# Feed-forward output projection by block products: seven for eight, in four chunks

## The chip, the core and the metric

The kernel runs on one core of a Trainium2 chip. The metric is device microseconds of one launch, lower is better; the number for a version is the median over several runs. A profile is one further execution, recorded by the hardware profiler.

## What is computed

One layer of a decoder: attention (MLA) over a prompt of 512 tokens and a batch of 8 single-token samples with paged caches, a chunked gating mixer, an output projection `w_o`, then the feed-forward part, then a gated per-layer embedding. Weights are shared by the two groups, and the kernel puts both side by side as 520 token columns. What the change touches is the last line of `conv_ffn`:

```python
def conv_ffn(hn, hist, w_ff_in, conv_w, conv_b, w_ff_out):
    a = hn @ w_ff_in                      # 1024 -> 2 x 2816
    ap = jnp.concatenate([hist, a], axis=1)
    c = conv_b
    for k in range(CONV_W):               # three taps along the tokens
        c = c + conv_w[k] * ap[:, k:k + T]
    g, up = c[..., :D_FF], c[..., D_FF:]
    return (jax.nn.silu(g) * up) @ w_ff_out, ...   # 2816 -> 1024
...
    h = h + f
    gate = sigmoid(rmsnorm(h) @ w_ple_gate)        # 1024 -> 1024
    e = rmsnorm(p_emb @ w_ple_proj)                # 256 -> 1024
    h = h + gate * e
```

All data are float32.

## The kernel before

**Layout.** Activations stand transposed: features on the 128 partitions, the 520 tokens as columns, in two halves of 260 (`HT`). The residual `x` is four tiles of two feature blocks each, so eight blocks `m`. `D_FF` is 22 tiles of 128 (`NFF`).

**Three matmuls for one.** Each float32 operand is split into a high part (cast to the type fp32r of the profile rows) and a low part (the rest): `split` (line 132 and after) makes the high part on ScalarE (line 135, or 137 with a scale) and the low part by a subtraction on VectorE (line 130, or 143 with a scale). `mm3` (lines 145 to 148) then adds high x high, high x low and low x high into the same PSUM tile: three matmuls of 128 x 128 weights by 260 columns.

**Weights.** `wq_add` puts every weight block of the kernel into one list of units, in the order of use. `wload` brings a unit from memory into one of three raw buffers `WR` by a DMA on SyncE's queue (line 190). `wget(i)` returns unit i split into two `W` tiles (there are nine), and beforehand splits the units up to three further ahead. So eight `W` tiles are in use or made ready.

**Feed-forward.** The 22 tiles of `D_FF` are taken in thirds of 8, 8 and 6 (`THIRDS`, line 907). For each tile f of a third, two input projections (gate and up: 48 matmuls each) run by `proj`; `ff_half` (line 1054) evacuates one with the normaliser (line 1057), convolves it (ScalarE line 1059, VectorE lines 1060 to 1062); the SiLU is line 1097, the product with up line 1098, and the result is split as the right-hand operand of the output projection (line 1099). After the last tile of a third the output projection runs over its tiles: for each of eight blocks m a `proj` of nf k-tiles (nf x 6 matmuls), added into `x[m]` from PSUM by VectorE (line 1111). The first two blocks leave out their last k-tile until both are otherwise done (`proj_two`), which gives the last activation time.

**End section.** In the last third three `e_mm` (the embedding projection, 12 matmuls each, copied out on ScalarE at line 1077 and squared for a norm, line 217, added up by VectorE at line 221) come ahead of the output projection, and the other five between its blocks. Behind each add into `x[m]` the finished block is split for the gate projection with a scale (lines 137, 143) and squared for its norm. The gate stage follows: eight projections of 48 matmuls, the last in two column halves into PSUM tiles of their own (`proj_apart`), with evacuation at line 1137.

**PSUM.** `mm()` tiles hold two banks (three tiles), `ms()` tiles one bank (two tiles).

**Order.** The code names the engine of each operation. The tile framework plans the order of each engine's instructions at build time: an instruction whose inputs come later by the plan may be overtaken by one that is written behind it. At run time each engine takes its instructions in the planned order, and waits on semaphores. A tile from a ring (`W`, `WR`, PSUM) can be written again once all readers of its earlier content have finished.

**GpSimd** works earlier, in the attention stages, among them on the rotary products of lines 466 to 469, which VectorE and GpSimd share by token blocks, and on low parts of the cache pages (line 130 with GpSimd as its engine). It has no work in the feed-forward.

Of the kernel before, what the change touches and what calls it, by code (L numbers as in the profile page):

```python
# [8 lines left out]
F32R = mybir.dt.float32r  # L9
# [11 lines left out]
NT = T + B  # L21
# [9 lines left out]
NFF = 22  # L31
# [8 lines left out]
NAT = 8  # L40
KRQ = 2
EF = 3
PF = 2
# [3 lines left out]
def trunk_step(ctx: ExitStack, tc: tile.TileContext, I, O):  # L47
# [125 lines left out]

    wunits = []
    wraw = []
    wsrc = {}
    wtiles = []

    def wq_add(src, w, l="v", scale=None, tile_=W, parts=1):

        cuts = [(i * w // parts, (i + 1) * w // parts) for i in range(parts)]
        wunits.append((src, l, scale or [None] * parts, tile_, cuts))
        return len(wunits) - 1

    def wload(i):
        while len(wraw) <= i:
            src, _, _, _, cuts = wunits[len(wraw)]
            wraw.append(WR())
            for a, b in cuts if len(wraw) == 1 else [(0, cuts[-1][1])]:
                nc.sync.dma_start(wraw[-1][:, a:b], src[:, a:b])  # L190

    def wget(i, ahead=3):
        while len(wtiles) < min(i + 1 + ahead, len(wunits)):
            n = len(wtiles)
            wload(n)
            _, l, scale, tile_, cuts = wunits[n]
            wh, wl = tile_(F32R), tile_(F32R)
            for (a, b), sc in zip(cuts, scale):
                split(wh[:, a:b], wl[:, a:b], wraw[n][:, a:b], scale=sc, l=l)
            wsrc[n], wraw[n] = wraw[n], None  # L200
            wtiles.append((wh, wl))
        return wtiles[i]
# [703 lines left out]

    THIRDS = [(0, 8), (8, 8), (16, 6)]
    k_o = [wq_add(I["w_o"][i], 1024) for i in range(8)]
    k_fi, k_fo, k_pp = {}, {}, {}
    for th, (f0, nf) in enumerate(THIRDS):  # L910
        for f in range(f0, f0 + nf):
            for m in (f, NFF + f):
                k_fi[m] = wq_add(I["w_ffi"][m], 1024)
        for m in range(8):
            if th == 2 and m in (0, PF):
                k_pp[m > 0] = wq_add(I["w_pp"][int(m > 0)], 1024)
            k_fo[th, m] = wq_add(I["w_ffo"][th][m], nf * 128)
    k_pg = [wq_add(I["w_pg"][m], 1024) for m in range(8)]
# [18 lines left out]
    def halves(v):  # L937
        return v.rearrange("p (b t) -> p b t", b=2)
# [114 lines left out]

    def ff_half(m, ps):
        a = abuf[acnt[0] % NA]
        acnt[0] += 1
        nc.vector.tensor_mul(halves(a[:, 2:]), ps[:, :, 0:HT], halves(rstd_b))  # L1057
        c = A()
        nc.scalar.activation(c[:, 0:T], a[:, 2:T + 2], AF.Identity, scale=cw[:, m, 2:3], bias=cw[:, m, 3:4])  # L1059
# [9 lines left out]
    def e_mm(m):  # L1069
# [8 lines left out]
        ne.add(e[m])  # L1078

    hph, hpl = [], []  # L1080
    for th, (f0, nf) in enumerate(THIRDS):
        acth, actl = pair(nf // 2, F32R), pair(nf // 2, F32R)
        for f in range(nf):
            if th == 2 and f == 3:
# [5 lines left out]
            ks = k_fi[f0 + f], k_fi[NFF + f0 + f]  # L1090
            pg, pu = proj_two(ks, hn, 8) if f0 + f == 0 else (proj(k, hn, 8) for k in ks)
            if f0 + f == 0:
                nc.scalar.preload_act_table_set("natural_log_exp_and_others")
                nf_.finish(rstd_b)
            g = ff_half(f0 + f, pg)
            u_ = ff_half(NFF + f0 + f, pu)
            nc.scalar.activation(g, g, AF.Silu)
            nc.vector.tensor_mul(g, g, u_)  # L1098
            split(acth[f // 2][:, f % 2], actl[f // 2][:, f % 2], g)
        if th == 2:  # L1100
            for m in range(EF):
                e_mm(m)

        def act(kt):
            return acth[kt // 2][:, kt % 2], actl[kt // 2][:, kt % 2]

        first = proj_two([k_fo[th, m] for m in range(2)], act, nf)
        for m in range(8):
            ps = first[m] if m < 2 else proj(k_fo[th, m], act, nf)
            xv = x[m // 2][:, m % 2]  # L1110
            nc.vector.tensor_add(halves(xv), halves(xv), ps[:, :, 0:HT])
            if th == 2:
                if m % 2 == 0:
                    hph += pair(1, F32R)
                    hpl += pair(1, F32R)
                split(hph[m // 2][:, m % 2], hpl[m // 2][:, m % 2], xv, scale=g_pl[:, m:m + 1])
                np_.add(xv)
                if m + EF < 8:
                    e_mm(m + EF)
    nc.sync.dma_start(O["conv"], convb)  # L1120
# [23 lines left out]
def _layout(inp):  # L1144
# [63 lines left out]
    wo = g["w_ff_out"][0]  # L1208
    for i, (f0, nf) in enumerate([(0, 8), (8, 8), (16, 6)]):
        a[f"w_ffo{i}"] = tiles(wo[f0 * 128:(f0 + nf) * 128]).reshape(8, 128, nf * 128)  # L1210
    pe = np.concatenate([g["p_prompt"][0, 0], g["p_sample"][0, :, 0]], 0)
# [35 lines left out]
```

## Time and profile before

| | |
|---|---|
| runs, median (lowest to highest of 3) | 922.03 us (921.96 to 923.37) |
| profiled execution | 920.34 us, of which the span 918.6 |
| TensorE clock granted, mean | 0.99 |
| feed-forward with its end section | 560 to 868 us of the span |
| thirds' output projections | about 570.5 to 616.6, 708.9 to 755.2, 824 to 867 |
| gate stage | 868 to 918.6 |

How to read it: a profile row names an engine, a source line of the kernel before, the operation, `output<-inputs` by the program's tile names, the shapes, and how often. On the timeline the first two numbers are the start (us from the span's start) and the duration; in brackets stands how long the engine had been idle before it, and what it waited for. PE is TensorE (PEld its weight loads), DVE VectorE, ACT ScalarE, POOL GpSimd, SP SyncE. A matmul is shown for longer than the distance to the next, since matmuls are pipelined; the distance of starts is what counts.

### The profile page before, as it was taken

How to read it: one execution, taken by the hardware profiler on the slowest of the kernel's cores; microseconds unless marked ns; L12 is line 12 of the kernel's file. 1: busy time of each engine (PE TensorE's matmuls, PEld its weight loads, DVE VectorE, ACT ScalarE, POOL GpSimd, SP SyncE). 2: the span in 40 equal slices, each digit the busy share in tenths (PEclk: the TensorE clock that was granted, in tenths of full speed). 3: DMA queues.
4: the chain of work that ended last, by engine and by line, in shares of the span. 5: the costliest groups of instructions: out<-in, count | busy, mean ns of one | idle time of the engine just before them, and what ended most of it. 6: DMA issues, size and time to landing. Idle time of an engine off the chain costs nothing.

```text
span 918.6 us, 20633 instructions
## 1 busy us (share of the span) xinstructions
PE 892.9 (97%) x7799; PEld 846.5 (92%) x7799; DVE 660.2 (72%) x1133; ACT 503.0 (55%) x1188; POOL 204.7 (22%) x208
## 2 busy tenths in 40 slices
PE   7998999999999999989999999999999999999997
PEld 5896878888898888979999999999999999999997
DVE  6579766669999999897668776337776337776775
ACT  6573368777877787864446443224444214455561
POOL 5004841127676667630000000000000000000000
PEclk9998999999999999989999999999999999999999
DMA  6332150352667556314233222322222222323311
GB/s 217 99 96 81 50 182 1 95 161 79 203 183 210 161 162 193 121 31 138 86 100 110 89 86 86 103 89 87 90 93 92 93 92 93 104 85 98 116 58 59
DMA packets 65204, 100.44 MB, mean 109 GB/s; under 512 B 13825, under 2 KB 47754, under 8 KB 65106
## 3 DMA queue, kind: packets, MB, share of 16 engines
q1 hardware_dynamic: 63058, 94.93, 32.3%
q0 software_dynamic: 2048, 4.20, 1.8%
q8 instruction: 62, 1.02, 0.5%
q14 instruction: 36, 0.29, 0.1%
HBM read 95.95 MB, written 3.15 MB: 108 GB/s over the span
## 4 chain that ended last, share of the span: by engine, by line
PE 82%; DVE 7%; ACT 3%; DMA 2%; issue 2%; SPq 2%; POOL 1%; DVEq 0%; ACTq 0%
PE mm L146 24%; PE mm L148 24%; PE mm L147 23%; DVE ss L752 2%; PE ms L816 2%; PE ms L693 2%; SPq L601 1%; POOL xs L280 1%; DMA u<-pages 1%; DVE g L157 1%; DMA a<-xT 1%; PE ms L153 1%; PE mm L678 1%; PE ms L641 1%; PE mm L658 1%
## 5 line engine op out<-in xcount | busy, mean ns | idle before, releaser
L146 PE MATMUL mm<-u,w 128*128 128x260 f32 x1392 | 395.2, 284 | 0.0
L148 PE MATMUL mm<-u,w 128*128 128x260 f32 x1392 | 394.3, 283 | 0.0
L147 PE MATMUL mm<-u,w 128*128 128x260 f32 x1392 | 393.4, 283 | 0.0
L148 PEld LDWEIGHTS mm<-u,w 128*128 128x128 f32 x1392 | 262.0, 188 | 0.3 <-issue 0.2
L147 PEld LDWEIGHTS mm<-u,w 128*128 128x128 f32 x1392 | 262.1, 188 | 0.2
L146 PEld LDWEIGHTS mm<-u,w 128*128 128x128 f32 x1392 | 261.8, 188 | 0.4 <-PE mm L148 0.2
L130 DVE TENSOR_TENSOR w<-wr,w 128x1024 fp32r<-128x1024 f32 (+1 forms) x94 | 112.8, 1201 | 104.2 <-issue 54.3
L752 DVE TENSOR_REDUCE ss<-sq 128x8 f32<-128x512 f32 x256 | 166.6, 679 | 14.1 <-ACT sq L750 12.2
L750 ACT ACTIVATE sq<-mm 128x512 f32<-128x512 f32 x256 | 153.6, 614 | 34.7 <-PE mm L148 21.1
L135 ACT CAST w<-wr 128x1024 fp32r<-128x1024 f32 (+1 forms) x94 | 96.5, 1031 | 138.1 <-PE mm L148 127.3
L146 PE MATMUL mm<-wuk,a 128*128 128x260 f32 x416 | 124.8, 300 | 3.9 <-ACT raw L751 3.4
L148 PE MATMUL mm<-wuk,a 128*128 128x260 f32 x416 | 119.0, 286 | 0.0
L147 PE MATMUL mm<-wuk,a 128*128 128x260 f32 x416 | 118.6, 285 | 0.0
L146 PEld LDWEIGHTS mm<-wuk,a 128*128 128x128 f32 x416 | 79.4, 191 | 7.8 <-ACT raw L751 6.4
L147 PEld LDWEIGHTS mm<-wuk,a 128*128 128x128 f32 x416 | 79.6, 191 | 0.0
L148 PEld LDWEIGHTS mm<-wuk,a 128*128 128x128 f32 x416 | 79.4, 191 | 0.0
L588 POOL DMA_INDIRECT wr<-krT,idx x64 | 62.1, 971 | 11.4 <-issue 6.3
L1059 ACT ACTIVATE a<-abuf,cst 128x512 f32<-128x512 f32 x44 | 35.9, 816 | 39.3 <-DVE abuf L1057 39.2
L1060 DVE SCALAR_TENSOR_TENSOR a<-abuf,cst,a 128x512 f32<-128x512 f32 x44 | 33.1, 752 | 25.4 <-ACT a L1059 25.1
L130 POOL TENSOR_TENSOR a<-u,a 128x512 fp32r<-128x512 f32 x34 | 45.5, 1339 | 25.8 <-ACT a L714 13.0
L751 ACT COPY raw<-mm 128x8 f32<-128x8 f32 x256 | 45.9, 179 | 0.0
L135 ACT CAST u<-a 128x520 fp32r<-128x520 f32 x24 | 14.8, 626 | 43.4 <-DVE a L1098 43.3
(306 smaller groups left out, 1339.3 us busy)
## 6 DMA issues: line engine op xcount, KB each, us to landing
wr<-w_ffi SPq DMA_DIRECT2D x44, 512.0 KB, 3.3
u<-pages SPq DMA_DIRECT2D x152, 128.0 KB, 2.3
w<-pages SPq DMA_DIRECT2D x104, 128.0 KB, 2.4
wr<-w_ffo SPq DMA_DIRECT2D x16, 512.0 KB, 3.3
wr<-w_o SPq DMA_DIRECT2D x8, 512.0 KB, 4.3
wr<-w_pg SPq DMA_DIRECT2D x8, 512.0 KB, 3.2
wr<-w_ffo SPq DMA_DIRECT2D x8, 384.0 KB, 3.4
a<-xT SPq DMA_DIRECT2D x8, 260.0 KB, 7.2
```

The lines of the kernel that those rows point to most:

```text
L130: return (nc.vector if eng == "v" else nc.gpsimd).tensor_sub(dl, src, dh.bitcast(F32))
L135: nc.scalar.copy(dh, src)
L146: nc.tensor.matmul(out, lh, rh, start=start, stop=False)
L147: nc.tensor.matmul(out, lh, rl, start=False, stop=False)
L148: return nc.tensor.matmul(out, ll, rh, start=False, stop=stop)
L588: nc.gpsimd.indirect_dma_start(krT[:, g * 128:(g + 1) * 128], None, I["krT"], bass.IndirectOffsetOnAxis(ap=idx.bitcast(U32)[:, b * 8 + g:b ...
L693: nc.tensor.matmul(po[:, 0:256], v[:, ks], pt_[:, k * 256:k * 256 + 256], start=(k == 0), stop=(k == qb))
L750: squares.append(nc.scalar.activation(u3(sq, 2, 256), ps[:, :, 0:256], AF.Square))
L751: nc.scalar.copy(raw[:, c * 8:c * 8 + 8].rearrange("p (a h) -> p a h", a=2), ps[:, :, 256:260])
L752: nc.vector.tensor_reduce(ss[:, c * 8:c * 8 + 8], sq.rearrange("p (h d) -> p h d", d=DN), axis=AX.X, op=ALU.add)
L1059: nc.scalar.activation(c[:, 0:T], a[:, 2:T + 2], AF.Identity, scale=cw[:, m, 2:3], bias=cw[:, m, 3:4])
L1060: nc.vector.scalar_tensor_tensor(c[:, 0:T], a[:, 1:T + 1], cw[:, m, 1:2], c[:, 0:T], op0=ALU.mult, op1=ALU.add)
```

## The change

The output projection is written as 2 x 2 block products. The left operand of a quad q is the weights of two output blocks (m = 2q, 2q + 1) by pairs of k-tiles, the right operand the activations of such pairs by the two column halves. Strassen's scheme in Winograd's form gets the four result blocks from seven products: with the weight blocks A11, A21, A12, A22 it uses A11, S1 = A21 + A22, S2 = S1 - A11, S3 = A11 - A21, A12, A22, S4 = A12 - S2, and on the right B11, T1, T2, T3, B21, T4, B22.

- The 22 tiles are taken in chunks of 6, 6, 6 and 4 (`CHUNKS`).
- Weights: a quad has two loads and seven units of cost 1 (one `W` tile holds high and low part, half a width each); the other units have cost 2. `wget` looks ahead up to a cost of 8. The sums S1 to S4 run on GpSimd (six-tile chunk: 384 columns each, four-tile chunk: 256), into the `sq` ring of three tiles.
- Right-hand operand: class `Right` gets each finished activation; for a pair of tiles it makes four differences on GpSimd (260 columns each) and splits seven operands. It lies in up to eight `U` tiles and in `G` tiles.
- Results: each product has a PSUM bank of its own, `ms` for the products P0, P2 and P6, `mm` for the others. ScalarE copies the first, VectorE adds six of them up by seven additions of 260 columns, and four further additions into `x` run on GpSimd.
- The first tile of the next chunk (`ahead`) is projected ahead of the chunk's products, and its convolution and product run between the quads.
- In the last chunk the split of `x`, its norm and the `e_mm` follow each quad, two blocks at a time. `w_ff_out` is stored in the new order ahead of the launch.

```diff
+QUAD = ("A11", "S1", "S2", "S3", "A12", "A22", "S4")
+CHUNKS = ((0, 6), (6, 6), (12, 6), (18, 4))
...
+        def make(name):
+            a = wraw[n]
+            b = wraw[n + 1] if name != "A11" else None
+            a11, a21 = a[:, 0:w], a[:, w:2 * w]
+            if name[0] == "A":
+                v = a11 if name == "A11" else b[:, 0:w] if name == "A12" else b[:, w:2 * w]
+            else:
+                v = s[name] = Q()[:, 0:w]
+                if name == "S1":
+                    nc.gpsimd.tensor_add(v, a21, b[:, w:2 * w])
+                elif name == "S2":
+                    nc.gpsimd.tensor_sub(v, s["S1"], a11)
+                elif name == "S3":
+                    nc.gpsimd.tensor_sub(v, a11, a21)
+                else:
+                    nc.gpsimd.tensor_sub(v, b[:, 0:w], s["S2"])
+            t = W(F32R)
+            wh, wl = t[:, 0:w], t[:, w:2 * w]
+            split(wh, wl, v)
...
-    def wget(i, ahead=3):
-        while len(wtiles) < min(i + 1 + ahead, len(wunits)):
+    def wget(i, ahead=None):
+        while len(wtiles) < len(wunits):
             n = len(wtiles)
...
+            make, ld, cost = wunits[n]
+            if n > i and (n > i + ahead if ahead is not None else sum(u[2] for u in wunits[i:n + 1]) > 8):
+                break
+            wload(ld)
+            wtiles.append(make())
...
+        def add(self, g):
+            lo, hi = slice(0, HT), slice(HT, NT)
+            if self.g is None:
+                self.g = g
+                self.put("B11", g[:, lo])
+                nc.gpsimd.tensor_sub(g[:, lo], g[:, hi], g[:, lo])
+                self.put("T1", g[:, lo])
+                return
+            p, self.g = self.g, None
+            self.put("B21", g[:, lo])
+            self.put("B22", g[:, hi])
+            nc.gpsimd.tensor_sub(p[:, hi], g[:, hi], p[:, hi])
+            nc.gpsimd.tensor_sub(p[:, lo], g[:, hi], p[:, lo])
+            self.put("T2", p[:, lo])
+            nc.gpsimd.tensor_sub(g[:, lo], g[:, lo], p[:, lo])
+            self.put("T3", p[:, hi])
+            self.put("T4", g[:, lo])
+
+    def products(k, right, x0, x1):
...
+        def prod(i, name, ps):
+            wh, wl = wget(k + i)
+            ops = right.ops[name]
+            for kt, (rh, rl) in enumerate(ops):
+                ks = slice(kt * 128, kt * 128 + 128)
+                mm3(ps[:, 0:HT], wh[:, ks], wl[:, ks], rh, rl, kt == 0, kt == len(ops) - 1)
+
+        t, c = A(), A()
+        p1, u2 = t[:, lo], t[:, hi]
+        ps1, pa = ms(), mm()
+        prod(0, "B11", ps1)
+        nc.scalar.copy(p1, ps1[:, 0:HT])
+        nc.gpsimd.tensor_add(x0[:, lo], x0[:, lo], p1)
+        prod(1, "T1", pa[:, 0])
+        ps6 = ms()
+        prod(2, "T2", ps6)
+        nc.vector.tensor_add(u2, ps6[:, 0:HT], p1)
+        nc.vector.tensor_add(c[:, lo], pa[:, 0, 0:HT], u2)
+        nc.gpsimd.tensor_add(x0[:, hi], x0[:, hi], c[:, lo])
+        prod(3, "T3", pa[:, 1])
+        nc.vector.tensor_add(u2, pa[:, 1, 0:HT], u2)
+        nc.vector.tensor_add(c[:, hi], pa[:, 0, 0:HT], u2)
+        nc.gpsimd.tensor_add(x1[:, lo], x1[:, lo], u2)
+        nc.gpsimd.tensor_add(x1[:, hi], x1[:, hi], c[:, hi])
+        pb = mm()
+        prod(4, "B21", pb[:, 0])
+        nc.vector.tensor_add(x0[:, lo], x0[:, lo], pb[:, 0, 0:HT])
+        prod(5, "T4", pb[:, 1])
+        nc.vector.tensor_add(x1[:, lo], x1[:, lo], pb[:, 1, 0:HT])
+        ps3 = ms()
+        prod(6, "B22", ps3)
+        nc.vector.tensor_add(x0[:, hi], x0[:, hi], ps3[:, 0:HT])
...
+    ahead = ff_tile(0)
+    for c, (f0, nf) in enumerate(CHUNKS):
+        end = f0 + nf == NFF
+        right = Right(6 if end else 8)
+        right.add(run(ahead))
+        for f in range(f0 + 1, f0 + nf):
...
+            right.add(run(ff_tile(f)))
+        if end:
             for m in range(EF):
                 e_mm(m)
+        else:
+            ahead = ff_tile(f0 + nf)
+        for q in range(4):
+            xq = [x[q][:, i] for i in range(2)]
+            products(k_fo[c, q], right, *xq)
+            if ahead[0]:
+                ahead[0].pop(0)()
+            if end:
...
+                for i in range(2):
+                    m = 2 * q + i
+                    split(hph[q][:, i], hpl[q][:, i], xq[i], scale=g_pl[:, m:m + 1])
+                    np_.add(xq[i])
+                    if m + EF < 8:
+                        e_mm(m + EF)
```

More of the change, by code (lines that the diff above doesn't have):

```diff
@@ L1208, in _layout @@
     wo = g["w_ff_out"][0]
[L1209 to L1210 removed]
+    for i, (f0, nf) in enumerate(CHUNKS):
+        w = tiles(wo[f0 * 128:(f0 + nf) * 128]).reshape(4, 2, 128, nf // 2, 2, 128)
+        a[f"w_ffo{i}"] = ac(w.transpose(0, 4, 2, 1, 3, 5).reshape(4, 2, 128, nf * 128))
     pe = np.concatenate([g["p_prompt"][0, 0], g["p_sample"][0, :, 0]], 0)
@@ L1230 @@
     O = {k: nc.dram_tensor("out_" + k, s, F32, kind="ExternalOutput").ap() for k, s in _OUTS.items()}
-    I["w_ffo"] = [I["w_ffo0"], I["w_ffo1"], I["w_ffo2"]]
+    I["w_ffo"] = [I[f"w_ffo{i}"] for i in range(len(CHUNKS))]
     with tile.TileContext(nc) as tc:
```

120 lines of the change are left out of this document (71 added, 49 removed).

## The prediction

> **What bounds it now.** I read the page's totals, slices and chain first, then the stages by windows.
>
> ```profile
> span 918.6 us, 20633 instructions
> PE 892.9 (97%) x7799; PEld 846.5 (92%) x7799; DVE 660.2 (72%) x1133; ACT 503.0 (55%) x1188; POOL 204.7 (22%) x208
> POOL 5004841127676667630000000000000000000000
> PEclk9998999999999999989999999999999999999999
> PE 82%; DVE 7%; ACT 3%; DMA 2%; issue 2%; SPq 2%; POOL 1%; DVEq 0%; ACTq 0%
> ```
>
> TensorE is 82% of the chain that ended last. In the second half, where the feed-forward lies, its clock is full and GpSimd (POOL) does nothing at all. Windows (length, then PE, PEld, DVE, ACT, POOL busy), first one third's output projection, then eight tiles of the input projection, the end section, the gate stage, and all of the feed-forward:
>
> ```profile
> 570.50:616.60 46.10, 46.10 (x386) 46.10 (x385) 15.27 (x17) 8.51 (x9) 0.00 (x0) 1.00 0.28 92
> 616.60:708.90 92.30, 92.30 (x765) 92.30 (x765) 66.80 (x95) 40.77 (x63) 0.00 (x0) 1.00 0.28 92
> 820.00:868.00 48.00, 48.00 (x404) 48.00 (x403) 33.10 (x45) 28.70 (x45) 0.00 (x0) 1.00 0.32 105
> 868.00:918.60 50.60, 45.67 (x373) 45.08 (x372) 31.80 (x49) 19.13 (x25) 0.00 (x0) 0.98 0.17 63
> 560.00:868.00 308.00, 308.00 (x2560) 308.00 (x2559) 184.81 (x252) 120.25 (x179) 0.00 (x0) 1.00 0.28 94
> ```
>
> From 560 to 868 us PE never pauses, and VectorE (DVE) is 33% busy in the output projection against 72% in the input projection. One matmul is worth 308.00 / 2560 = 0.1203 us. So in this stretch a matmul taken away is time gained, as long as no other engine needs longer than PE.
>
> **What goes.** The output projection has 8 tiles x 22 k-tiles x 2 column halves x 3 = 1056 matmuls of 260 columns. The change runs 4 quads (two output tiles each) x 7 products x 11 pairs of k-tiles x 3 = 924, of the same shape. That is 132 fewer, 132 x 0.1203 = 15.9 us. A product puts 9 matmuls in a row into one PSUM bank instead of 3; the last gate tile already puts 24 in a row, and its two halves are evacuated 2.88 us apart, 0.120 us each, so the rate holds:
>
> ```profile
> 910.83 0.43 DVE L1137 TENSOR_TENSOR a<-ms,rstd_b 128x260 f32<-128x260 f32 x1
> 913.71 0.43 DVE L1137 TENSOR_TENSOR a<-ms,rstd_b 128x260 f32<-128x260 f32 x1 [1.08 <-PE ms L148]
> ```
>
> **What comes.** Prices of DVE and ScalarE (ACT) operations, and of POOL's two-input operations when DVE leaves it alone:
>
> ```profile
> 839.80 0.96 DVE L130 TENSOR_TENSOR w<-wr,w 128x768 fp32r<-128x768 f32 x1 [0.37 <-PE mm L147]
> 840.68 0.69 DVE L1111 TENSOR_TENSOR u<-u,mm 128x520 f32<-128x520 f32 x1
> 842.61 0.76 DVE L143 SCALAR_TENSOR_TENSOR u<-u,cst,u 128x520 fp32r<-128x520 f32 x1 [1.24 <-ACT u L137]
> 843.28 1.31 DVE L221 TENSOR_TENSOR g<-g,g 128x520 f32<-128x520 f32 x2
> 822.67 0.75 DVE L1060 SCALAR_TENSOR_TENSOR a<-abuf,cst,a 128x512 f32<-128x512 f32 x1 [0.87 <-ACT a L1059]
> 821.58 0.23 DVE L1062 SCALAR_TENSOR_TENSOR a<-abuf,cst,hb 128x8 f32<-128x8 f32 x1
> 839.92 0.84 ACT L135 CAST w<-wr 128x768 fp32r<-128x768 f32 x1 [1.22 <-PE mm L148]
> 824.98 0.63 ACT L135 CAST u<-a 128x520 fp32r<-128x520 f32 x1
> L796 POOL TENSOR_TENSOR raw<-raw,g x8: 737/750/977, 213.3 to 423.2; 128x256 f32<-128x256 f32 x8
> L130 POOL TENSOR_TENSOR a<-w,a x18: 1277/1292/1308, 227.5 to 406.0; 128x512 fp32r<-128x512 f32 x18
> ```
>
> A DVE operation starts 0.08 before the one ahead of it has ended (two of 520 columns take 1.31, so 0.62 each; 768 columns 839.80 to 840.68, 0.88). Along these lines 384 columns cost DVE 0.48 in a row (0.56 alone), 256 or 260 cost 0.35 (0.43), 1024 cost 1.15, line 143 0.67, a tap of the convolution 0.67. ACT: 384 columns 0.51, 256 or 260 0.41. POOL, between 0.75 for 256 and 1.29 for 512: 384 columns 1.02, 260 0.76.
>
> A quad of a six-tile chunk is 63 matmuls, 7.6 us of PE. In that time POOL has four block sums (4 x 1.02) and four adds into x (4 x 0.76), 7.1. DVE has seven low parts (7 x 0.48) and seven PSUM adds (7 x 0.35), 5.8, and in the first two quads also the next tile's convolution, 2 x 0.67 + 0.15 = 1.5, in the first its evacuation 0.62, in the third its product 0.62. ACT has 7 x 0.51 + 0.41 = 4.0, which hides. The blocks are made for the quad after, so three quads of a chunk are heavy; in the fourth, DVE splits three input-projection units instead (3 x 1.15) and POOL only adds. DVE over the three heavy ones: 7.9 + 7.3 + 6.4 = 21.6 against PE's 22.7. Taken singly, each engine fits, by little. (The right-hand sums and splits lie in the input projection: for two tiles DVE has seven parts of 0.35 for two of 0.62, 0.6 a tile more on 66.8 in 92.3, and POOL four of 0.76; that hides.)
>
> They do not run singly. Around 81 to 91 us POOL and DVE both do operations on two SBUF inputs:
>
> ```profile
> 82.42 1.49 POOL L468 TENSOR_TENSOR u<-u,g 128x512 f32<-128x512 f32 x1
> 83.87 1.40 POOL L469 TENSOR_TENSOR u<-u,g 128x256 f32<-128x256 f32 x1
> 85.23 5.51 POOL L466 TENSOR_TENSOR u<-u,g 128x512 f32<-128x512 f32 x1
> 81.46 1.54 DVE L468 TENSOR_TENSOR u<-u,g 8x512 f32<-8x512 f32 x1
> 82.92 1.25 DVE L469 TENSOR_TENSOR u<-u,g 8x256 f32<-8x256 f32 x1
> 84.11 0.67 DVE L466 TENSOR_TENSOR u<-u,g 128x512 f32<-128x512 f32 x1
> ...
> 85.47 0.27 DVE L370 TENSOR_TENSOR g<-u,g 8x128 f32<-8x128 f32 x1
> ...
> 89.42 0.41 DVE L469 TENSOR_TENSOR u<-u,g 128x256 f32<-128x256 f32 x1
> ```
>
> DVE's 512 columns take 1.54 where they take 0.67 at 84.11: they waited for POOL. POOL's L468 in turn can only have worked from 83.00, where that DVE operation ended, to 83.91: 0.91 of it excludes DVE. L469, from 84.78 to 85.27, has 0.49 of that kind. So a POOL operation of 384 columns holds DVE's two-input work off for 0.70, one of 260 for 0.50; a heavy quad has 4 x 0.70 + 4 x 0.50 = 4.8 of it. But from 85.47 to 89.83 DVE runs its operations in a row undelayed, and POOL's one takes 5.51. So a wait of DVE for POOL is not certain. PSUM adds have one SBUF input; no row shows them waiting, and I take them as free.
>
> Six-tile chunks: the port is in POOL's hands 4.8 of some 8 us, 0.6 of the time, with 0.3 of the turn left on average: 0.17 for each of 25 two-input DVE operations (nine, nine, seven) is 4.3 if DVE arrives at random, 2.1 if half go by unhindered as at 85.47. DVE then needs 25.9 or 23.7 against 22.7. What may lag: the seventh product's PSUM tile is needed again two products into the next quad (18 x 0.1203 = 2.2, less the add and the hand-over, 1.6 left). Loss a chunk 1.6 or 0; three chunks 4.8 or 0, I take 2.4. POOL's own lag (some 1 us a quad of such turns on 7.1) has more cover: a block is made seven products, 7.6 us, ahead, less its own 1.02 + 0.51 + 0.56. Were that gone, it would cost 1.2 a chunk.
>
> The last chunk (four tiles) is where DVE is longest. From the end of the last input projection to the last split of x, PE has eight e tiles (12 matmuls each) and 28 products of 6: 264 x 0.1203 = 31.7. DVE has the last tile's evacuation, convolution and product 2.7, five right-hand low parts 1.8, 22 block low parts 7.7, 28 PSUM adds 9.8, eight splits of x 5.4, twelve of the fourteen adds of two norms 7.4, three gate units 3.4: 38.2. Of that 4.3 may come late (the gate's first six k-tiles, 36 matmuls, need only earlier parts of x): 33.9, 2.2 over PE. ACT, busy for 28.7 in the same window before, loses eight casts of 0.84 and gains 31 operations of 0.41, 34.7 at most, under DVE. Then the start: the third product needs T2.
>
> ```profile
> 821.34 0.59 ACT L1077 COPY e<-mm 128x520 f32<-128x520 f32 x1 [0.66 <-PE mm L148]
> 824.25 0.70 DVE L1098 TENSOR_TENSOR a<-a,a 128x520 f32<-128x520 f32 x1
> ```
>
> The first e tile, 1.4 us of PE, is copied at 821.3, so the input projection ends near 819.9 and the product of gate and up near 825.0, 5.1 later. Two POOL subtractions, a cast and a low part (2 x 0.76 + 0.41 + 0.43) make 7.5; three e tiles and two products cover 5.8. Of the 1.7 I take 1.0, since a fourth e tile may be drawn ahead (no row bounds that better). Last, POOL has 32 operations, 16 us of the port in some 36: 0.11 for each of 53 two-input operations, 5.8 or half, 2.9; I take 4.4. Loss 2.2 + 1.0 + 4.4 = 7.6. With no wait for POOL 3.2 would be left; if PSUM adds waited too, 28 x 0.11 = 3.1 would come on top.
>
> Two moves without price, each with its cover: weight loads on SP's queue. The second load of a quad waits for the third block sum of the quad two before (three raw buffers), and later loads queue behind it. A 384 KB load lands in 3.4 us:
>
> ```profile
> wr<-w_ffo SPq DMA_DIRECT2D x8, 384.0 KB, 3.4
> ```
>
> It starts about 6 us into a quad's 7.6 and is wanted 2.5 into the next, 4.1 later, and block sums can be 5.5 late. The deferred last k-tile of each third is replaced by a whole tile's input projection (11.5 us of PE) before the products, longer than the 7.5 above. Without these covers: 3.4 a quad, and 7.5 a chunk.
>
> Sum: -15.9 + 2.4 + 7.6 = -5.9. The profiled execution took 920.34 us (918.6 span and 1.7 around it), which becomes 914.4; the runs' median, 922.03, lies 1.7 above it and becomes 916.1.
>
> **Rivals.** *POOL's turns fall on DVE (slower).* Every turn delays DVE but for what PSUM adds and evacuations hide. A chunk's heavy quads: 21.6 + 14.4 - 8.0 = 28.0, less 22.7 and 1.6, 3.7 lost; three, 11.1. The last: 38.2 + 16.0 - 9.8 - 4.3 + 1.0 - 31.7 = 9.4. Less the 15.9, +4.6, 926.6; with half hidden 23.1 + 14.3, +21.5, 943.5. It decides from a mean wait of about 0.16 us for a two-input DVE operation (3 x 1.3 + 3.2 + 53 x 0.16 = 15.6). For it: 1.54 and 1.25 above. Against: the row of undelayed operations. The Trainium skill, page "SBUF — State Buffer", section "SBUF: two separate sides", says that GpSimd and a DVE operation with two SBUF inputs share one port pair as an exclusive lock, held for the whole instruction, while the loser blocks fully. By that rule alone the sum would be this rival's, not mine. The trace agrees that they exclude each other (0.91 after 83.00); at 85.23 the loser was shut out for many instructions, not one.
>
> *Queues in source order (slower).* In the source the next quad's blocks stand between this quad's adds. In order, POOL's round would be x add, S1, S2, then the cast, low part and two DVE adds behind S2 (1.9), x add, S3, 1.5, two x adds, S4: 10.6 a quad. 3 x 3.0 - 1.6 = 7.4 a chunk; 22.2 + 7.6 - 15.9 = +13.9, 935.9. Against it, each engine's order here is not the source's: the copy of an e tile (here in an `a` tile), written behind the split of x, runs ahead of it.
>
> ```profile
> 841.35 0.59 ACT L1077 COPY a<-mm 128x520 f32<-128x520 f32 x1 [0.59 <-PE mm L148]
> 841.84 0.73 ACT L137 ACTIVATE u<-u,cst 128x520 fp32r<-128x520 f32 x1
> ```
>
> *All hidden (faster).* DVE wins the port each time: only 3.2 at the end is lost, 909.3; were that gone too, 906.1. For it: DVE at 33% in the output projection, POOL at 0. Against: 38.2 against 31.7.
>
> *Saving handed back (no change).* The wait lies at its turning point, 922. That the change doesn't save PE time at all needs a lower matmul rate, which the 2.88 us speak against; it is in this case.
>
> **Numbers.** Forecast 0.36 (911.5 to 920.2), all hidden 0.18 (below), no change 0.14, POOL's turns 0.26, source order 0.06. A measurement here tells apart about 0.2%, 1.8 us. So faster 0.54, same 0.14, slower 0.32. The range 908 to 931 leaves out 0.06 below and some 0.13 above; the forecast's own range is 911.5 to 920.2.
>
> **What would show it.** PE: 924 matmuls in the products, 0.12 apart inside each. Pauses should stand ahead of the third product of a quad, released by DVE, about 1 us a chunk in the first three and 7 in the last, where DVE is near 100% busy. POOL's 384-column sums last over 1.02 and DVE's 384-column low parts over 0.56, by 0.1 to 0.15 in the mean; 0.16 and more means no gain. If pauses stand ahead of a product whose weights are late, the lookahead failed; if none stand at the end, DVE's 38.2 is wrong.

## The result and the profile after

The changed kernel takes 955.82 us (median of 4, 954.17 to 956.41) against 922.0 us on the same chip (921.17 to 923.37): a ratio of 1.0362, 95% interval 1.0344 to 1.0381. The forecast of 916.1 was wrong in sign, and its range of 908 to 931 does not hold the time. Of the cases in it, "POOL's turns fall on DVE" came out, at more than its highest price (943.5). Of the runs told below, one of the kernel with memsets (2924.35 us) and one with the last chunk plain on VectorE (1684.96 us) were far longer than the others, and the ratios leave them out.

Totals, GpSimd's slices, clock and chain of the profiled execution after:

```profile
span 953.5 us, 21147 instructions
PE 896.0 (94%) x7667; PEld 841.6 (88%) x7667; DVE 775.3 (81%) x1364; ACT 544.5 (57%) x1347; POOL 375.4 (39%) x380
POOL 4007821246666657610002466125731356226300
PEclk9998999999999999999999999999999998998999
PE 56%; DVE 25%; ACT 5%; issue 5%; POOL 5%; DMA 2%; SPq 0%; DVEq 0%; ACTq 0%; POOLq 0%
```

The 132 matmuls are gone (7667 for 7799), but VectorE's share of the chain is 25% where it was 7%. Windows of the profile after (length, then PE, PEld, DVE, ACT, POOL busy, granted clock, DMA share, GB/s): the products of the first chunk, the input projection behind them, most of the last chunk, and all of the feed-forward:

```profile
554.00:594.80 40.80, 33.26 (x255) 32.09 (x254) 38.21 (x63) 18.55 (x36) 26.47 (x26) 0.96 0.34 105
600.00:664.00 64.00, 64.00 (x531) 64.00 (x530) 53.01 (x78) 28.74 (x58) 17.80 (x17) 1.00 0.21 67
...
857.00:904.00 47.00, 36.90 (x249) 34.37 (x249) 41.92 (x75) 28.91 (x60) 24.88 (x30) 0.89 0.25 79
560.00:904.00 344.00, 313.47 (x2459) 307.81 (x2459) 292.02 (x464) 158.19 (x314) 147.85 (x150) 0.97 0.27 86
```

Where PE was busy all the time before, it now rests in the products, and there its clock falls under 1 too (0.96, 0.89), while VectorE is busy for 38.21 of 40.80 us. An account can be made from the starts of all matmuls after 480 us: a distance over 0.26 us between two starts is a pause, one of 0.15 to 0.26 is stretched, by the half clock or by a short gap; each counts less the 0.12 of a normal distance. Pauses are 38.7 us (before: 1.0), stretched distances 13.1 (1.0). Of the 13.1, 9.0 lie in the six stretches of the feed-forward, 23.9 us in all, for which the trace has a granted clock of 0.5; the rest are short gaps. So 37.7 + 12.1 - 15.9 = +33.9, and the measured difference is +33.8. By place the pauses are 8.6, 7.7 and 7.6 in the three chunks of six and 14.3 in the last.

What PE waits for, in the products:

```profile
PE mm L148 <- DVE a L1210: 20.5, 11, 2.7
PE ms L148 <- ACT u L137: 2.9, 1, 2.9
PE ms L148 <- DVE a L1209: 2.2, 1, 2.2
```

Line 1210 is VectorE's sum of the second product (P1) and `u2`. PE begins a quad's products in the order P0, P1, P2, P4, P6, P3, P5; P3 writes the other half of P1's PSUM tile, and PE waits for the read of the first half. VectorE's groups in the first chunk's heavy quads (count, busy us, mean ns, idle before), then GpSimd's sums over the whole feed-forward:

```profile
L132 DVE TENSOR_TENSOR w<-wr,w 128x384 fp32r<-128x384 f32 x8 | 7.5, 941 | 0.0
L132 DVE TENSOR_TENSOR w<-sq,w 128x384 fp32r<-128x384 f32 x9 | 6.5, 760 | 0.0
L1112 DVE SCALAR_TENSOR_TENSOR a<-abuf,cst,a 128x512 f32<-128x512 f32 x2 | 3.1, 1544 | 0.0
...
L1209 DVE TENSOR_TENSOR a<-ms,a 128x260 f32<-128x260 f32 x4 | 1.7, 418 | 0.0
L1113 DVE SCALAR_TENSOR_TENSOR a<-abuf,cst,a 128x512 f32<-128x512 f32 x2 | 1.6, 820 | 0.0
L1114 DVE SCALAR_TENSOR_TENSOR a<-abuf,cst,hb 128x8 f32<-128x8 f32 x2 | 1.3, 649 | 0.0
```

```profile
L213 POOL TENSOR_TENSOR sq<-wr,wr 128x384 f32<-128x384 f32 x12 | 16.1, 1344 | 21.0 <-DMA wr<-w_ffo 16.9 <-DVE w L132 1.9 <-DVE a L1210 1.3
L215 POOL TENSOR_TENSOR sq<-sq,wr 128x384 f32<-128x384 f32 x12 | 15.8, 1320 | 7.6 <-DVE a L1114 7.1
L219 POOL TENSOR_TENSOR sq<-wr,sq 128x384 f32<-128x384 f32 x12 | 14.9, 1238 | 6.8 <-DVE w L132 6.8
...
L217 POOL TENSOR_TENSOR sq<-wr 128x384 f32<-128x384 f32 x12 | 12.3, 1025 | 7.8 <-DVE w L132 7.8
```

Low parts with two SBUF inputs last 0.94 and 0.76 for some 0.55, one tap 1.54 and the other 0.82 for 0.75; the adds with a PSUM input (line 1209) keep their 0.42. GpSimd's sums are longer than the 1.02 of the forecast, but for S3. How a pause comes about is seen on the timeline of one (start, duration), with GpSimd's operations of that time ahead of VectorE's:

```profile
577.29 1.19 POOL L1216 TENSOR_TENSOR u<-u,a 128x260 f32<-128x260 f32 x1
578.45 1.06 POOL L1205 TENSOR_TENSOR u<-u,a 128x260 f32<-128x260 f32 x1
580.07 1.20 POOL L219 TENSOR_TENSOR sq<-wr,sq 128x384 f32<-128x384 f32 x1 [0.56 <-DVE w L132]
...
577.80 1.10 DVE L132 TENSOR_TENSOR w<-wr,w 128x384 fp32r<-128x384 f32 x1
578.83 2.86 DVE L132 TENSOR_TENSOR w<-sq,w 128x384 fp32r<-128x384 f32 x3
581.62 0.69 DVE L1144 TENSOR_TENSOR a<-a,a 128x520 f32<-128x520 f32 x1
582.23 0.42 DVE L1209 TENSOR_TENSOR a<-ms,a 128x260 f32<-128x260 f32 x1
582.56 0.54 DVE L132 TENSOR_TENSOR w<-wr,w 128x384 fp32r<-128x384 f32 x1
583.03 0.42 DVE L1210 TENSOR_TENSOR a<-mm,a 128x260 f32<-128x260 f32 x1
...
583.50 0.58 PE L148 MATMUL mm<-u,w 128*128 128x260 f32 x1 [2.73 <-DVE a L1210]
```

Four low parts take from 577.80 to 581.62, 3.8 us, where alone they take 4 x 0.47 = 1.9. The first ends at 578.90, 0.42 after a GpSimd operation, the last at 581.69, 0.42 after another. PE stands still for the 2.73 us to 583.50, when line 1210 has at last had its turn.

### The profile page after: what moved, and what is told of

Same layout as the page of the kernel before. It is cut to its first block, busy times and chain, and to the rows that moved or that the text cites. A ratio compares the mean times of both kernels' runs of the same rounds, so it can differ in the third digit from the quotient of the medians.

```text
span 953.5 us, 21147 instructions
## 1 busy us (share of the span) xinstructions
PE 896.0 (94%) x7667; PEld 841.6 (88%) x7667; DVE 775.3 (81%) x1364; ACT 544.5 (57%) x1347; POOL 375.4 (39%) x380
## 3 DMA queue, kind: packets, MB, share of 16 engines
q1 hardware_dynamic: 64210, 94.93, 31.8%
## 4 chain that ended last, share of the span: by engine, by line
PE 56%; DVE 25%; ACT 5%; issue 5%; POOL 5%; DMA 2%; SPq 0%; DVEq 0%; ACTq 0%; POOLq 0%
PE mm L148 16%; PE mm L150 14%; PE mm L149 14%; DVE w L132 7%; DVE a L1112 3%; DVE ss L797 2%; DVE a L1113 2%; PE ms L861 2%; PE ms L738 2%; DVE a L1114 1%; DVE u L132 1%; DVE abuf L1106 1%; DVE a L1144 1%; PE ms L148 1%; POOL u L1215 1%
## 5 line engine op out<-in xcount | busy, mean ns | idle before, releaser
L148 PE MATMUL mm<-u,w 128*128 128x260 f32 x1172 | 337.7, 289 | 25.1 <-DVE a L1210 20.5
L150 PE MATMUL mm<-u,w 128*128 128x260 f32 x1172 | 335.0, 286 | 0.0
L149 PE MATMUL mm<-u,w 128*128 128x260 f32 x1172 | 334.7, 286 | 0.0
L148 PEld LDWEIGHTS mm<-u,w 128*128 128x128 f32 x1172 | 222.9, 190 | 29.7 <-DVE a L1210 22.8
L149 PEld LDWEIGHTS mm<-u,w 128*128 128x128 f32 x1172 | 223.8, 191 | 0.4 <-DVE u L145 0.2
L150 PEld LDWEIGHTS mm<-u,w 128*128 128x128 f32 x1172 | 223.7, 191 | 0.5 <-issue 0.2
L132 DVE TENSOR_TENSOR w<-wr,w 128x1024 fp32r<-128x1024 f32 (+2 forms) x118 | 124.3, 1055 | 30.1 <-PE mm L149 13.9
L137 ACT CAST w<-wr 128x1024 fp32r<-128x1024 f32 (+2 forms) x118 | 96.3, 818 | 79.8 <-PE mm L150 57.1
L1176 POOL TENSOR_TENSOR a<-a 128x260 f32<-128x260 f32 x11 | 10.9, 992 | 121.9 <-DVE u L132 121.9
L137 ACT CAST u<-a 128x260 fp32r<-128x260 f32 (+1 forms) x62 | 24.2, 415 | 60.1 <-DVE a L1144 36.3
L1112 DVE SCALAR_TENSOR_TENSOR a<-abuf,cst,a 128x512 f32<-128x512 f32 x44 | 42.6, 968 | 11.8 <-ACT a L1111 11.3
```

Of the source, the lines that this page charges most:

```text
L132: return (nc.vector if eng == "v" else nc.gpsimd).tensor_sub(dl, src, dh.bitcast(F32))
L137: nc.scalar.copy(dh, src)
L148: nc.tensor.matmul(out, lh, rh, start=start, stop=False)
L149: nc.tensor.matmul(out, lh, rl, start=False, stop=False)
L150: return nc.tensor.matmul(out, ll, rh, start=False, stop=stop)
L1112: nc.vector.scalar_tensor_tensor(c[:, 0:T], a[:, 1:T + 1], cw[:, m, 1:2], c[:, 0:T], op0=ALU.mult, op1=ALU.add)
```

## The experiments

Theories after the result. *Port*: GpSimd's operations that read SBUF hold VectorE's two-input operations off, and PE waits for VectorE. *Hand-over*: P3 waits only because it shares a PSUM tile with P1. *VectorE's own load*: the products need more of it than there is, with or without GpSimd. Later came *queue*: GpSimd's sums are late because they stand behind its adds, which wait for VectorE.

All the results first. "Loss" is the change against the kernel before on the same chip, plus what the missing matmuls are worth (132 x 0.1203 = 15.9, or 108 x 0.1203 = 13.0); pauses and stretched distances are counted as above, less the 1.0 of each before. In the trace of the kernel without block sums, of that with a tile between and GpSimd, and of both with the last chunk plain on VectorE, the granted clock never falls in the feed-forward, so there the last column is short gaps alone. (The expectations below call the whole of this column half clock.) The rows with 13.0 do the last chunk with eight plain products.

| kernel | us | before, same chip | ratio, 95% interval | loss | pauses | stretched |
|---|---|---|---|---|---|---|
| changed kernel | 955.82 | 922.00 | 1.0362 (1.0344 to 1.0381) | 49.7 | 37.7 | 12.1 |
| block sums left out | 924.43 | 921.48 | 1.0023 (1.0011 to 1.0036) | 18.8 | 14.8 | 3.1 |
| PSUM tiles apart | 958.90 | 921.48 | 1.0396 (1.0372 to 1.0421) | 53.3 | 42.1 | 13.7 |
| all sums on VectorE | 933.71 | 921.48 | 1.0127 (1.0099 to 1.0155) | 28.1 | 19.5 | 8.1 |
| memsets for block sums | 930.23 | 921.48 | 1.0087 (1.0056 to 1.0117) | 24.6 | 17.9 | 4.7 |
| block sums on VectorE | 931.40 | 921.28 | 1.0100 (1.0071 to 1.0130) | 26.0 | 17.7 | 6.7 |
| adds into x on VectorE | 946.20 | 921.28 | 1.0274 (1.0245 to 1.0304) | 40.8 | 31.8 | 8.2 |
| GpSimd, last chunk plain | 940.46 | 922.39 | 1.0200 (1.0163 to 1.0236) | 31.1 | 23.9 | 7.3 |
| the same, tile between | 922.09 | 922.39 | 1.0001 (0.9982 to 1.0020) | 12.7 | 11.3 | 1.2 |
| VectorE, last chunk plain | 919.14 | 921.28 | 0.9973 (0.9955 to 0.9990) | 10.9 | 8.2 | 1.9 |
| the same, tile between | 909.94 | 921.28 | 0.9884 (0.9854 to 0.9914) | 1.7 | 0.0 | 1.0 |

**Block sums left out.** S1 to S4 are not formed; raw blocks are split in their place.

```diff
-                v = s[name] = Q()[:, 0:w]
-                if name == "S1":
...
+                v = {"S1": a21, "S2": a11, "S3": a21, "S4": b[:, 0:w]}[name]
```

> The four GpSimd sums of weight blocks of each quad are left out; S1 to S4 are split from the raw blocks A21, A11, A21, A12 instead. All else is the changed kernel (955.8 us, TensorE gaps 38 us and half clock 12 us more than before). If GpSimd's turns at the SBUF port delay VectorE and so TensorE, the low parts of 384 columns come back from 0.81 to near 0.56 us and the time to 925 to 935 us. If the third result product waits for VectorE's adds because two products share one PSUM tile, whatever GpSimd does, the time stays above 945 us and the waits for line 1210 stay near 20 us.

31 us of the 50 lost go with GpSimd's 64 block sums, work that PE never reads directly. A loss of 18.8 stays, so the sums are most of it and not all. The time lies just under the 925 to 935 of the port theory; the low parts come back to 0.62 us and not to 0.56. P1 and P3 share their tile here as before, and PE's wait of 20.5 us in front of P3 is down to 5.2:

```profile
PE mm L148 <- DVE a L1202: 5.2, 10, 0.7
```

**PSUM tiles apart.** P1 and P3, P4 and P5 in tiles of their own.

```diff
-        ps1, pa = ms(), mm()
+        ps1, pa = ms(), [mm()[:, 0], mm()[:, 0]]
...
-            pb = mm()
+        pb = [mm()[:, 0], mm()[:, 0]]
```

> P1 and P3, and P4 and P5, get PSUM tiles of their own instead of the two halves of one; nothing else. If the wait of P3 for the read of P1's half (20.5 us on TensorE behind the add that stood at line 1210) is the cause, most of these 20 us and of the 12 us of half clock go: 925 to 935 us. If VectorE is simply late because of GpSimd's turns, the wait only moves to another product or to a weight block: 948 to 956 us.

The wait of PE that led the list before has another line now:

```profile
PE mm L148 <- DVE a L1213: 20.7, 13, 3.1
```

It has the same size, and the kernel loses 3.6 us more than the changed one, above both expected ranges. Four such tiles a quad have to come from a ring of three, so PE now waits for a tile to come free: this run puts one hand-over in the place of another. What speaks against the hand-over as the cause is the run before it, where the shared tile stayed and three quarters of the wait went.

**All sums on VectorE.** Block sums, right-hand differences and adds into x move from GpSimd to VectorE.

```diff
-                    nc.gpsimd.tensor_add(v, a21, b[:, w:2 * w])
+                    nc.vector.tensor_add(v, a21, b[:, w:2 * w])
```

(and so for the other eleven additions of the output projection)

> All of GpSimd's sums and adds of the output projection run on VectorE instead. VectorE gets 16 more operations of 0.34 to 0.48 us in a pair of quads, 9.1 us of own work in a heavy quad for 5.8, and no port to share. Port theory: a GpSimd operation costs VectorE 0.5 to 0.7 us of waiting, as much as doing it itself, so the time comes out between 940 and 960 us, no slower than the changed kernel. If GpSimd's work were free of VectorE, 29 us of added VectorE work would show: 970 us and more.

It is 22 us faster than the changed kernel, with 172 operations more on VectorE, and below both expected ranges: taken together, the sums and adds cost more on GpSimd than VectorE needs to do them. Its totals, the low parts, and three starts of line 1209, which stands once in a quad:

```profile
PE 889.8 (96%) x7667; PEld 837.3 (90%) x7667; DVE 772.9 (83%) x1536; ACT 545.2 (59%) x1347; POOL 204.3 (22%) x208
```

```profile
L132 DVE TENSOR_TENSOR w<-sq,w 128x384 fp32r<-128x384 f32 x48 | 26.4, 551 | 0.0
...
L132 DVE TENSOR_TENSOR w<-wr,w 128x384 fp32r<-128x384 f32 x36 | 19.4, 552 | 0.3
```

```profile
565.39 0.42 DVE L1209 TENSOR_TENSOR a<-ms,a 128x260 f32<-128x260 f32 x1
...
575.93 0.42 DVE L1209 TENSOR_TENSOR a<-ms,a 128x260 f32<-128x260 f32 x1
...
585.65 0.43 DVE L1209 TENSOR_TENSOR a<-ms,a 128x260 f32<-128x260 f32 x1
```

VectorE was busy for 775.3 us with 1364 operations, and is busy for 772.9 with 1536. Giving 172 operations to GpSimd had taken nothing off VectorE: it was occupied as long, waiting for GpSimd. The second and third heavy quads last 10.5 and 9.7 us, and that is what the prediction's prices make of them: 7.3 and 6.4 of own work, with 4 x 0.48 for the sums and 4 x 0.35 for the adds 10.6 and 9.7. (The first, from 557.69 on, lasts 7.7 and falls short of its price.)

**Memsets for block sums.** Each block sum is replaced by two memsets on GpSimd into the same tile, so GpSimd is occupied but reads no SBUF; the sums are left out of the result.

```diff
+                for _ in range(2):
+                    nc.gpsimd.memset(v, 0.0)
```

> Each GpSimd sum of two weight blocks is replaced by two memsets of the same tile: GpSimd is about as long busy (0.8 us for 1.0) and the split still waits for it, but it reads nothing from SBUF. The block sums are left out of the result. Port theory: low parts near 0.56 us and a time like the kernel without the sums (within 5 us). If what costs is only that the blocks come late from GpSimd, the time stays near 955 us.

```profile
L132 DVE TENSOR_TENSOR w<-sq,w 128x384 fp32r<-128x384 f32 x48 | 26.6, 574 | 1.1 <-ACT w L137 0.8
L132 DVE TENSOR_TENSOR w<-wr,w 128x384 fp32r<-128x384 f32 x36 | 23.9, 665 | 0.0
```

The low parts that follow the memsets take 574 ns, near the 551 without GpSimd; that those at 665 still meet the adds into x fits, but was not shown. The time, 930.23, is 5.8 us above the kernel without sums, a little more than the 5 expected. Of the 31 us between the changed kernel and the one without sums, 6 come with a GpSimd that only writes (24.6 against 18.8). The other 25 go with its reading, but for what the memsets save otherwise: two take about 0.78 us, less than a sum's 1.02 to 1.34, and they wait for no weight block. The Trainium skill, page "SBUF — State Buffer", section "SBUF: two separate sides", says that a VectorE operation with two SBUF inputs is locked out only by a GpSimd operation that reads SBUF; these 574 ns agree.

**Block sums on VectorE, and adds into x on VectorE.** The two halves of GpSimd's work, moved singly.

```diff
-        nc.gpsimd.tensor_add(x0[:, lo], x0[:, lo], p1)
+        nc.vector.tensor_add(x0[:, lo], x0[:, lo], p1)
```

> The changed kernel with the block sums of the weights (S1 to S4) on VectorE; GpSimd keeps the adds into x and the differences of the right-hand operand. Port theory (every column that GpSimd reads holds VectorE's two-input operations off): the sums are 12 x 2.8 + 4 x 2.0 = 41.6 us of the port, the adds into x 16 x 2.0 = 32; of the 22 us between the changed kernel and the one with all on VectorE, 57% go, 943, between 939 and 948. Rival (GpSimd's queue: a sum stands behind an add into x that waits for VectorE, so the weights come late): with the sums gone from the queue all of it goes, 932 to 936.

> The changed kernel with the adds into x on VectorE; GpSimd keeps the block sums of the weights and the differences of the right-hand operand. Port theory: 32 of 73.6 us of port time go, 43% of 22 us, 946, between 942 and 951. Rival (GpSimd's queue): the sums no longer stand behind adds that wait for VectorE, so the weights come in time, 932 to 936.

The first, 931.40, misses the port theory's 943 and comes near the queue theory's 932 to 936; the second, 946.20, meets the port theory's 946 and not the queue theory. So neither holds for both: the price is not in proportion to GpSimd's port time, and late sums are not the whole of it. (In the changed kernel none of PE's listed waits is for a weight tile.) With the adds and right-hand differences alone on GpSimd the loss is 26.0, against 28.1 with all on VectorE: these 108 operations cost nothing there that could be measured, and take 4.5 us off VectorE's busy time (768.4 for 772.9). VectorE's rows with the block sums on VectorE (only the adds into x and the right-hand differences on GpSimd), then those with the adds on VectorE (the block sums and the differences on GpSimd):

```profile
L1112 DVE SCALAR_TENSOR_TENSOR a<-abuf,cst,a 128x512 f32<-128x512 f32 x44 | 34.6, 786 | 12.4 <-ACT a L1111 12.3
...
L132 DVE TENSOR_TENSOR w<-sq,w 128x384 fp32r<-128x384 f32 x48 | 27.6, 584 | 0.0
L132 DVE TENSOR_TENSOR w<-wr,w 128x384 fp32r<-128x384 f32 x36 | 23.4, 650 | 0.0
```

```profile
L1112 DVE SCALAR_TENSOR_TENSOR a<-abuf,cst,a 128x512 f32<-128x512 f32 x44 | 38.0, 865 | 11.8 <-ACT a L1111 11.5
...
L132 DVE TENSOR_TENSOR w<-sq,w 128x384 fp32r<-128x384 f32 x48 | 33.4, 710 | 1.5 <-ACT w L137 1.5
L132 DVE TENSOR_TENSOR w<-wr,w 128x384 fp32r<-128x384 f32 x36 | 25.2, 700 | 0.0
```

The block sums hold VectorE off more than the adds do: 710 and 865 against 584 and 786. That the adds into x run while VectorE does additions from PSUM, and so meet few two-input operations, fits this, but was not shown apart.

**The last chunk plain, with VectorE or with GpSimd.** The last four tiles are done by eight products, as in the kernel before.

```diff
-    for c, (f0, nf) in enumerate(CHUNKS):
+    for c, (f0, nf) in enumerate(CHUNKS[:-1]):
...
+    for m in range(8):
+        ps = first[m] if m < 2 else proj(k_fo[c, m], act, nf)
+        xv = x[m // 2][:, m % 2]
+        nc.vector.tensor_add(halves(xv), halves(xv), ps[:, :, 0:HT])
```

> All sums of the output projection are on VectorE, as in the kernel that gave 933.71, and the last chunk (four tiles) is done with the plain eight products, as in the kernel before; three chunks keep the seven. This gives back 24 of the 132 matmuls... worked out: the last chunk has 8 x 4 x 2 x 3 = 192 matmuls plain and 168 by blocks, so 24 matmuls, 2.9 us, are added. Theory (VectorE's own load is what is left to pay in the last chunk: 11.7 us of pauses and 6.6 of half clock): those 18 us go, the chunks keep 3.2 each, so 933.7 + 2.9 - 18.3 + some 2 for the pauses that the kernel before has at its end = 920, between 917 and 923. Rival (the end pays for something else, the late activation of the last tile or the order of e tiles and splits): the pauses stay, 933 to 937.

> The changed kernel, GpSimd's sums included, with the last chunk as eight plain products. Its 14.4 us of pauses and about 5 of half clock there go, 2.9 us of matmuls come back: 955.8 - 19 + 2.9 = 940, between 937 and 943, if the last chunk's loss is its own; the three chunks keep 8 each. If the last chunk's pauses were a lag handed on from the chunks before, the kernel keeps some of them, 945 and up.

Both came as VectorE's load and a chunk's own loss had it. The block products of the last chunk cost 28.1 - 10.9 = 17 us where VectorE does all, and 49.7 - 31.1 = 19 with GpSimd. So the last chunk loses as much whichever of the two engines does the sums. In the kernel without block sums 9.5 of its 14.3 us of pauses stay, so their turns are the smaller part of it.

**A tile between the quads.** In each chunk, a second tile's input projection is put ahead of the third quad; with all on VectorE, then with the sums on GpSimd.

```diff
-        ahead = ff_tile(f0 + nf)
+        ahead = [ff_tile(f0 + nf)]
         for q in range(4):
+            if q == 2:
+                ahead.append(ff_tile(f0 + nf + 1))
```

> Like the kernel with the last chunk plain, and in each of the three chunks a second tile's input projection (11.5 us of TensorE, some 7 to 8 of VectorE) is put between the second and the third quad of products. Theory (VectorE falls behind by a little in each heavy quad, and the lag adds up until TensorE waits): a pause for VectorE to catch up takes most of the 3.2 us a chunk away, 5 to 9 us less than with the last chunk plain alone, 911 to 916. Rival (each quad pays by itself, because of the PSUM tiles or the late first sums): no difference over 2 us between the two.

> As the changed kernel with the last chunk plain, and in each chunk a second tile's input projection between the second and the third quad, as in the kernel that gave 909.94, but with all block sums and adds on GpSimd. Port theory: two heavy quads put VectorE 2 x 4.4 us behind (12.0 against TensorE's 7.6), the tile between gives back about 4, the third puts it 4.4 behind again, so the pauses shrink but stay, 3 to 5 us a chunk, with half clock 922 to 930. Rival (GpSimd's sums are merely late, and any pause in the products lets them arrive): no pauses are left, 910 to 914.

The first, with nothing on GpSimd, beats both kernels: 909.94 us, a little better than expected, and 9.2 less than without the tile between. Its window over the feed-forward shows PE busy throughout, and VectorE at 88%:

```profile
560.00:870.00 310.00, 310.00 (x2560) 309.08 (x2560) 273.04 (x535) 161.39 (x295) 0.00 (x0) 1.00 0.32 100
```

A lag of VectorE added up over the heavy quads, and 11.5 us of PE work that asks less of VectorE let it catch up. With GpSimd the same tile brings more (31.1 to 12.7), and the time, 922.09, is at the lower end of the port theory's range, but this wait stays:

```profile
PE mm L148 <- DVE a L1217: 9.4, 12, 1.5
```

Two by two, the three chunks lose 31.1 and 12.7 with GpSimd, 10.9 and 1.7 without. In neither order is GpSimd's help, sums and adds together, worth its price.

**The port where VectorE has room.** The kernel before, with four additions on GpSimd behind each add into x, whose results nobody uses.

```diff
+            for w in (384, 384, 260, 260):
+                nc.gpsimd.tensor_add(Q()[:, 0:w], xv[:, 0:w], pad[:, 0:w])
```

> The kernel before, with work that nobody uses: behind each add into a block of x in the output projection (24 times) GpSimd does four additions, two of 384 and two of 260 columns, on that block and a tile of zeros, so per two blocks the same port time as a heavy quad of the changed kernel, 4.8 us, in 11.5 us. Port theory (it is VectorE's time that GpSimd takes, and only that): VectorE, 33% busy there, gets longer low parts (1.22 us alone for 1024 columns, 0.1 to 0.4 more), and the time stays, 920 to 924. Rival (GpSimd's traffic in SBUF slows TensorE's operands or the weight loads too): pauses of TensorE where VectorE is free, 5 us and more, 927 and up.

The time, 944.19 against 922.39 (ratio 1.0254, 1.0210 to 1.0299), is outside the port theory's 920 to 924. Its places tell more. Most of the first third's output projection, then VectorE's low parts in it, ahead of them those of the kernel before:

```profile
588.00:632.00 44.00, 44.00 (x368) 44.00 (x368) 18.25 (x19) 9.96 (x10) 29.99 (x32) 1.00 0.29 98
```

```profile
L130 DVE TENSOR_TENSOR w<-wr,w 128x1024 fp32r<-128x1024 f32 x9 | 11.0, 1225 | 30.9 <-issue 26.6 <-PE mm L147 4.4
...
L130 DVE TENSOR_TENSOR w<-wr,w 128x1024 fp32r<-128x1024 f32 x9 | 12.7, 1407 | 29.3 <-issue 24.9 <-PE mm L147 4.4
```

GpSimd works for 30 of 44 us, low parts rise from 1.22 to 1.41, and PE never pauses: here GpSimd's traffic does not touch TensorE, and where VectorE has room its turns cost nothing. Over the 2400 matmuls from the 4800th on, both kernels take 289.3 us. Then the end section and the gate stage, where VectorE has less room (busy for 29.81 of the 33.00 us from 853 to 886), lose the other 9.5, the longest pause being this, with what stands ahead of it:

```profile
886.01 1.75 DVE L130 TENSOR_TENSOR w<-wr,w 128x1024 fp32r<-128x1024 f32 x1
...
888.40 0.73 ACT L137 ACTIVATE u<-u,cst 128x520 fp32r<-128x520 f32 x1 [3.22 <-DVE u L1113]
...
889.18 0.58 PE L146 MATMUL mm<-u,w 128*128 128x260 f32 x1 [3.61 <-ACT u L137]
```

The pause ends a chain that starts at a low part of 1.75 us for 1.22. The first 12.6 us are lost ahead of the output projection, in the attention stages, where the two differ only by the larger ring of squares and the tile of zeros. Why is left open, so the total says nothing about the port.

## Why the prediction was wrong

**Right: the worth of a matmul.** 108 fewer should save 13.0, and 11.3 were measured where no pause was added (interval of the ratio: 7.9 to 13.5). The rate holds with nine matmuls in a row into one bank.

**Right: the work of VectorE and the kind of loss.** The heavy quad's own load, the free additions from PSUM (0.42 for 0.43), GpSimd's sums over 1.02 and low parts over 0.56 came as listed; of PE's listed waits in the products, none is for a weight load. The sign that the prediction set itself came too: 384-column low parts 0.16 and more over 0.56 "means no gain", and over the feed-forward they take 0.81 and 0.83:

```profile
L132 DVE TENSOR_TENSOR w<-sq,w 128x384 fp32r<-128x384 f32 x48 | 37.4, 808 | 1.5 <-ACT w L137 1.5
...
L132 DVE TENSOR_TENSOR w<-wr,w 128x384 fp32r<-128x384 f32 x36 | 29.9, 829 | 0.0
```

**Wrong: the mean wait of VectorE for a turn of GpSimd.** This is the step that failed. It had "0.3 of the turn left on average: 0.17" for each operation if VectorE arrives at random, half of that if half go by, and the sum took the middle of the two losses, which stands for some 0.13. In the window of the first chunk's heavy quads the two-input groups give, against 0.55 for the low parts with all on VectorE and the 0.75 and 0.23 that the prediction's rows give the taps and the eight columns, 8 x 0.39 + 9 x 0.21 + 2 x 0.79 + 2 x 0.07 + 2 x 0.42 = 7.6 over 23 operations: 0.33. That is two and a half times the value taken, and twice the 0.16 from which the prediction's own rival decided. With 25 x 0.33 = 8.2 the prediction's sum for a chunk becomes 21.6 + 8.2 - 22.7 - 1.6 = 5.5 instead of 0.8 (measured pauses: 7.6 to 8.6; the rest of them this sum does not give). That alone turns -5.9 into +8: 3 x 5.5 + 7.6 - 15.9. Halving the wait for the one row of operations that ran undelayed was a bad choice, but the full 0.17 would have been too low as well (1.6 a chunk). There one waiting GpSimd operation met a row of VectorE's; here GpSimd has several in a row of its own, and on the timeline above two of four low parts end 0.42 behind one of them. Why the mean is twice that of a random arrival was not shown apart.

**Wrong: PE's rest costs clock.** The prediction counted a pause at its length. 12.1 us more went to stretched distances, 9.0 of them at half the clock.

**Wrong: the last chunk.** Forecast 7.6, measured 19. VectorE is at 89% there (41.92 of 47.00) and not "near 100%", so the sum of its work is not the bound by itself: the waits in the chain (2.9 us for the cast of a right-hand part, 2.2 for line 1209) lie in a row with it. With all on VectorE the loss is 17, and without block sums 9.5 us of pauses stay, so better turns at the port would have saved only a part of it.

**Wrong: the place.** Pauses stand ahead of P3 more than ahead of the third product, since P3 comes behind the start of P6 in PE's order. In the run with tiles apart they stand elsewhere and the time is no better, so the place is not what made the loss.

**The rivals.** "POOL's turns fall on DVE" named the cause. Its 943.5 with half hidden was too low because it lacked the clock and took the end for a matter of sums. "All hidden" needed VectorE to win the port each time. "Queues in source order" had 935.9 from late sums: the run with the block sums on VectorE (931.40) would suit it, the one with the adds there (946.20) does not, and in the changed kernel PE waits for no weight tile.

## What to carry to other kernels

Operations moved to GpSimd can take nothing off VectorE if both read SBUF at that time: 172 of them here left it busy as long. Compare VectorE's busy time after with its operations counted, not GpSimd's share before. Where an engine has room on average but not in a stage, spreading the stage out (here one tile's projection between the quads) can be worth more than a helper: it brought 9.2 us, and with it the kernel gained 1.2% where the change as made cost 3.6%. And a forecast of pauses on TensorE must price the slow clock that can follow them.

## What the runs showed of the hardware

**The clock falls without a whole idle window.** The window behind the 2.73 us pause:

```profile
583.30:586.70 3.40, 3.20 (x15) 3.20 (x15) 2.99 (x7) 0.84 (x1) 1.08 (x2) 0.51 0.25 83
```

Half the clock for 3.4 us, matmuls 0.216 us apart instead of 0.120. The Trainium skill, page "TensorE: Matmul & The Clock Gate", section "Part 1: The HAM clock gate (the "warmup" mystery)", gives the slow state after at least one idle window of some 3.4 us; here less than that of rest was enough. Length alone does not decide it: a pause of 2.23 us (to 878.64) was followed by half the clock, those of 2.35 (to 571.35) and 2.30 (to 694.10) were not. In the kernel with GpSimd and a tile between, whose listed pauses stay at 1.5 us and under, the granted clock never falls in the feed-forward.

**An operation on 8 columns can wait too.** The 0.22 us operation of line 1114 takes 0.65 on average (of two) in the first chunk's heavy quads: the delay does not shrink with the operation's size.
